# First weight pairs of an encoder layer: plain products per tile pair and row half in place of half-depth Strassen

## The chip, the cores and the metric

The kernel runs on one core of a Trainium2 chip. The core has a matrix engine (TensorE, in the profile PE, with PEld for its weight loads), three elementwise engines (VectorE or DVE, ScalarE or ACT, GpSimd or POOL), and SyncE (SP), which here issues nearly all DMA transfers. Each engine runs its own instructions strictly in the order in which the build laid them down and waits on semaphores for the others. Products accumulate in PSUM, which has eight banks of 128 x 512 f32; everything else lives in SBUF. The metric is the device time of one execution in microseconds.

## The reference

One encoder layer over 1024 rows of width 2048, f32. A conditioning vector c gives shift and scale (the modulation), x is normalised by row and modulated, and the result h is multiplied with two wide weight matrices, `w_in` (4608 columns) and `w_merge` (4096 columns). What follows (attention over a window, pooling, gates, the output product) is the same in both kernels.

```python
mod = jax.nn.silu(c) @ w_ada + b_ada
shift, scale, gate = jnp.split(mod, 3, axis=-1)
h = rmsnorm(x, pre_g) * (1.0 + scale[:, None]) + shift[:, None]
proj = h @ w_in
...
g = jax.nn.sigmoid(h @ w_merge + b_merge)
```

## The kernel before, in words

**Tiling.** h is held turned: tile k (of 16) holds 128 of the 2048 columns of h on the partitions, and row half s (0 or 1) holds 512 of the 1024 rows: `xT[k, s]`. Weights come as pairs of 128 columns ("a weight pair", 256 columns, `ORDER` lists 34 of them). The contraction over 2048 is done in two passes, first over tiles 0 to 7 (`PART[0]`, results go to `part_d` in DRAM), then over tiles 8 to 15. Within a pass, tiles 2j and 2j+1 form tile pair j, j = 0 to 3.

**One product is three.** f32 values are split in a rounded part hi and a rest lo (`split`, lines 94 to 99: ACT writes hi, DVE subtracts and writes lo), and a product is hi*hi + hi*lo + lo*hi: three TensorE instructions of 128 x 128 by 128 x 512.

**Strassen.** For a weight pair, the 2 x 2 blocks (two tile halves by two column halves of the weights; two tile halves by two row halves of h) are multiplied with seven products instead of eight (`strassen`, lines 210 to 296). Its moving operands are the seven names in `MOVING`: the blocks B11, B21, B22 of h and the sums T1 to T4. B12 only enters through sums. For all four j a weight pair takes 7 x 3 x 4 = 84 TensorE instructions.

**The ramp.** To begin before all of h is there, the first `RAMP` = 4 weight pairs are done in two halves: first over j = 0, 1 for four pairs (results to `ramp_d`), then over j = 2, 3 (`ramp_gen`, lines 531 to 534, and the loops at 577 and 585), where the first half's results are loaded as `parts` and added. From the fifth pair on (`pass1`, line 602) all four j are done in one go, interleaved with side work (further modulation on DVE, sums of `w_out`). 22 pairs stand in the first call of `pass1`, the rest in the second.

**What leads to h.** `fetch_rows_of_x(s)` loads 16 tiles of 128 rows x 512 columns for half s. `norm_rows(si)` squares and sums a row block's four tiles (two on ACT, two on DVE) and makes a diagonal matrix `turn` of 1/rms. `turn_rows(s)` multiplies x with it on TensorE, which turns and scales x in one step (128 x 128 products into banks named XT), and copies the banks to `xT`. The modulation for tile pair j is a product of silu(c) (`scz`) with a 2048 x 512 block of `w_ada`: 16 TensorE instructions, four of which can work side by side on 32-column groups of the array (`modulation`, lines 443 to 463; bank GEMV). Then ACT copies the bank (`acc`), four small products add the groups (`sum_columns`, bank PM), and DVE forms `modc`. `modulate` applies it to `xT`, and `fill(j)` makes the 14 operands of tile pair j out of it.

**Order.** `fetch_rows_of_x` for both halves, the first raw weights, then `w_ada` for j = 0, 1, 2 in their own slots of the pool `big` (`ada_slots`) and for j = 3 through the ring `xa` of five buffers (`ada_tile`, two 256 KB loads each). All are loads on SyncE's one queue, at most eight on their way at a time. `claim` writes one column of the operands' slots early on POOL, so that they are taken from the pool ahead of need. The products of the modulation for j = 2 and 3 run in steps of two tiles between the Strassen products, pinned in the order in which they are written (`keep_in_program_order`). PSUM banks go by tags: mm, sc, at with two banks each, z0 and z1 (`SEEDED`) with one.

Of the kernel before, what the change touches and what calls it, by code (L numbers as in the profile page):

```python
# [42 lines left out]
def encoder_layer(ctx: ExitStack, tc: tile.TileContext, x, c, table, w_ada, b_ada, pre_g,  # L43
# [80 lines left out]
    RAMP = 4  # L124
# [3 lines left out]
    ramp_d = [dram.tile([256, S], F32, name=f"ramp_d{i}") for i in range(RAMP)]  # L128
# [51 lines left out]
    def load_raws(w, n0, rows, js):  # L180

        raws = []
        nj = len(js)
        joint = wp.tile([P, 2, nj, 256], F32, tag="raw", name=uid("raw"), bufs=4) if nj < 4 else None
        for kh in range(2):
            r = joint[:, kh] if nj < 4 else wp.tile([P, nj, 256], F32, tag="raw", name=uid("raw"), bufs=4)
            load(r, rows(w, js, kh)[:, :, n0:n0 + 256])
            raws.append(r)
        return raws
# [20 lines left out]
    def strassen(w, n0, rows, js, op, ev, finish, part=None, raws=None, ahead=False):  # L210
# [56 lines left out]
        if ahead:  # L267
            wts = iter(list(wts))
            yield
# [75 lines left out]
    ev_ctx = ExitStack()  # L345
    ev = ev_ctx.enter_context(pool("ev1", 9, side="right"))
    early = ExitStack()
    ep = early.enter_context(pool("early", side="right"))
    rows = ev.tile([P, 512], F32, tag="ev", name="rows")[0:104, 0:P]
# [16 lines left out]
    xT = {}  # L366
    for s in range(2):
        for k in PART[0]:
            if k % 4 == 3:
                xT[k, s] = rp.tile([P, 512], F32, name=f"xT{k}_{s}")  # L370
            else:
                xT[k, s] = slot("xT", F32)
                nc.gpsimd.memset(xT[k, s][:, 0:1], 0.0)
    xts, turn = {}, {}
# [7 lines left out]
    def norm_rows(si):  # L382
        ssq = ep.tile([P, 8], F32, tag="ssq", name=f"ssq{si}", bufs=4)
        for q in range(4):
            xt = xts[si, q]
            if q < 2:
                junk = bank("sc", "junk")
                nc.scalar.activation(junk, xt, AF.Square, accum_out=ssq[:, q:q + 1])
            else:
                junk = bank("at", "junk")  # L390
                nc.vector.scalar_tensor_tensor(junk, xt, 1.0, xt, op0=ALU.mult, op1=ALU.mult,
                                               accum_out=ssq[:, q:q + 1])
# [3 lines left out]
        turn[si] = ep.tile([P, P], F32, tag="turn", name=f"turn{si}", bufs=8)  # L396
        nc.vector.tensor_scalar(turn[si], ident, rstd[:, si:si + 1], None, op0=ALU.mult)

    def turn_rows(s):

        for q in range(2):
            banks = [bank(t, "XT1") for t in ("mm", "mm", *SEEDED)]
            for m in range(4):
                for j in range(4):
                    nc.tensor.matmul(banks[j][:, m * P:(m + 1) * P], xts[4 * s + m, q][:, j * P:(j + 1) * P],
                                     turn[4 * s + m], start=True, stop=True)
            for j in range(4):
                if j % 2 == 0:
                    nc.vector.tensor_copy(xT[q * 4 + j, s], banks[j])
                else:  # L410
                    nc.scalar.activation(xT[q * 4 + j, s], banks[j], AF.Copy)
# [22 lines left out]
    def ada_slots(j):  # L434
        tiles = []
        for kc in range(KT):
            tiles.append(slot("ada", F32, (P, 4, P)))
            load(tiles[kc].rearrange("p (g h) n -> p g (h n)", g=2),
                 w_ada[kc * P:(kc + 1) * P, 0:2 * D].rearrange("p (g n) -> p g n", g=2)
                 [:, :, j * 256:(j + 1) * 256])  # L440
        return tiles

    def modulation(j, tile_of, pin=False):

        st_ = {}

        def step(q):
            if q == 0:
                st_["pv"] = bank("at", "GEMV")
            pv = st_["pv"]  # L450
            for kc in (2 * q, 2 * q + 1):
                g = kc % 4 * 32
                ins = nc.tensor.matmul(pv[g:g + 32, :], scz[:, kc, :], tile_of(kc), start=kc < 4,
                                       stop=kc >= 12, tile_position=(0, g))
                if pin:
                    tc.keep_in_program_order(ins)
            if q == 7:
                acc = xa2.tile([P, 4, P], F32, tag="acc", name=uid("acc"), bufs=2)
                tc.keep_in_program_order(
                    nc.scalar.activation(acc, pv.rearrange("p (g n) -> p g n", g=4), AF.Copy))  # L460
                mod_columns(j, sum_columns(acc))

        return [lambda q=q: step(q) for q in range(8)]
# [30 lines left out]
    def modulate(eng, t, k):  # L494
        j, kh = k // 2, k % 2
        if eng is nc.scalar:
            eng.activation(t, t, AF.Identity, scale=modc[:, 1, kh, j:j + 1], bias=modc[:, 0, kh, j:j + 1])
        else:
            eng.tensor_scalar(t, t, modc[:, 1, kh, j:j + 1], modc[:, 0, kh, j:j + 1],
# [7 lines left out]
    def claim(j):  # L507

        for name in MOVING:
# [875 lines left out]
```

## Time and profile before

| what | value |
|---|---|
| device time, three runs | 2154.8, 2163.8, 2165.83 us (median 2163.8) |
| span of the profiled execution, first to last instruction | 2152.0 us |
| TensorE busy | 2098.7 us, 98% |
| DVE, ACT busy | 1539.9 us, 1129.6 us |
| DMA moved | 466.11 MB, mean 217 GB/s |

The median of the runs is 11.8 us above the span of the profiled execution; the execution that was profiled lies within its span and what the runs add around it.

How to read the profile: a timeline row has start and duration in us, the engine, the line of the kernel, the instruction, what it writes <- what it reads, the shape and how many such instructions were merged (xN). In brackets stand the idle time before and what ended it. A row of a table by stretches gives, for each engine, busy us and in parentheses the number of instructions, then TensorE's granted clock (1.00 is full), the mean busy share of the DMA engines and what they moved. A matmul's own duration is longer than the distance to the next, because matmuls overlap; the distance between starts is what counts. f32 matmuls (turning x, modulation) show two records for each instruction, the products of split operands one.

### The profile page before, as it was taken

To read this page: it belongs to the slowest core of one execution; us is meant where nothing else is said; L and a number is where in the kernel's file an instruction comes from. 1 tells how busy PE (TensorE), PEld (TensorE's weight loads), DVE (VectorE), ACT (ScalarE), POOL (GpSimd) and SP (SyncE) were. 2 spreads that over 40 slices of the span, in tenths; PEclk is the share of its full clock that TensorE was granted. 3 is DMA by queue.
4 is the path that set the end of the run, shared out by engine and by line. 5 is a ranking of instruction groups with operands and counts; after the bars stand their busy time and mean duration, and the time that the engine had idled before them with its cause. 6 is when DMAs were issued, how large, how long until landed. Compare 5 with 4: busy or idle time off the path is not lost.

```text
span 2152.0 us, 28951 instructions
## 1 busy us (share of the span) xinstructions
PE 2098.7 (98%) x9567; PEld 1716.3 (80%) x9567; DVE 1539.9 (72%) x2754; ACT 1129.6 (52%) x2124; POOL 7.4 (0%) x66
## 2 busy tenths in 40 slices
PE   6999999999999999999999999999999999999998
PEld 4588888887878888888888887888788887878886
DVE  5786666776547676777776878566967877879666
ACT  5654444443474546767765443334645544757654
POOL 0000000000000000000000000000000000000000
PEclk9999999999999999999999999999999999999999
DMA  9986566898666355545445765755654655686996
GB/s 333 290 277 202 188 203 212 296 316 271 227 224 206 118 175 199 171 158 186 161 150 189 220 223 192 238 177 177 229 175 156 230 167 175 207 287 215 303 314 226
DMA packets 303255, 466.11 MB, mean 217 GB/s; under 512 B 23882, under 2 KB 144866, under 8 KB 303104
## 3 DMA queue, kind: packets, MB, share of 16 engines
q1 hardware_dynamic: 301648, 462.02, 65.3%
q0 software_dynamic: 1120, 2.19, 0.3%
q8 instruction: 75, 1.23, 0.2%
q14 instruction: 76, 0.62, 0.1%
q10 hardware_dynamic: 336, 0.06, 0.0%
HBM read 340.41 MB, written 125.85 MB: 217 GB/s over the span
## 4 chain that ended last, share of the span: by engine, by line
PE 84%; DMA 8%; DVE 4%; ACT 2%; issue 1%; SPq 1%; DVEq 0%; ACTq 0%
PE Z L235 28%; PE X L235 18%; PE V L235 18%; DMA raw<-in_w_merge_dram 3%; PE Z L1131 2%; PE Z L1132 2%; PE Z L1133 2%; PE V L1131 1%; PE V L1133 1%; PE V L1132 1%; PE X L1132 1%; PE X L1133 1%; PE X L1131 1%; DVE wlo L96 1%; DMA xt<-in_x_dram 1%
## 5 line engine op out<-in xcount | busy, mean ns | idle before, releaser
L95 ACT ACTIVATE whi<-raw 128x512 fp32r<-128x512 f32 (+1 forms) x528 | 320.2, 610 | 509.1 <-PE Z L235 265.3
L96 DVE TENSOR_TENSOR wlo<-raw,whi 128x512 fp32r<-128x512 f32 (+1 forms) x528 | 346.9, 662 | 191.4 <-PE Z L235 114.6
L96 DVE TENSOR_TENSOR wlo<-wr,whi 128x512 fp32r<-128x512 f32 x224 | 150.9, 689 | 62.5 <-ACT whi L95 57.7
L95 ACT ACTIVATE whi<-wr 128x512 fp32r<-128x512 f32 x224 | 138.1, 628 | 99.6 <-DVE wlo L96 35.3
L102 DVE TENSOR_TENSOR raw<-raw,raw 128x512 f32<-128x512 f32 x80 | 55.2, 690 | 95.1 <-DMA raw<-in_w_merge_dram 73.2
L235 PE MATMUL V<-T3h,whi 128*128 128x512 f32 x336 | 92.3, 393 | 6.2 <-DVE u L102 6.2
L1057 ACT ACTIVATE gt<-gt,cols 128x512 f32<-128x512 f32 x64 | 46.0, 723 | 99.0 <-DMA gt<-proj_d 74.1
L235 PE MATMUL X<-B11h,whi 128*128 128x512 f32 x336 | 92.5, 393 | 3.2 <-DVE part L102 1.9
L235 PE MATMUL Z<-B22h,whi 128*128 128x512 f32 x336 | 92.8, 395 | 0.9 <-ACT u L290 0.9
L235 PE MATMUL Z<-T1h,whi 128*128 128x512 f32 x336 | 91.8, 392 | 0.9 <-ACT T1h L95 0.9
L235 PE MATMUL V<-T4h,whi 128*128 128x512 f32 x336 | 92.2, 392 | 0.0
L235 PE MATMUL X<-B11l,whi 128*128 128x512 f32 x336 | 92.1, 393 | 0.2 <-DVE B11l L96 0.2
L235 PE MATMUL X<-B11h,wlo 128*128 128x512 f32 x336 | 91.5, 392 | 0.0
L235 PE MATMUL Z<-T2h,whi 128*128 128x512 f32 x336 | 91.3, 391 | 0.0
L235 PE MATMUL Z<-T1l,whi 128*128 128x512 f32 x336 | 91.0, 390 | 0.1
L235 PE MATMUL Z<-B22l,whi 128*128 128x512 f32 x336 | 90.9, 390 | 0.0
L235 PE MATMUL X<-B21h,whi 128*128 128x512 f32 x336 | 90.9, 390 | 0.0
L235 PE MATMUL V<-T3l,whi 128*128 128x512 f32 x336 | 90.9, 390 | 0.0
L235 PE MATMUL V<-T4l,whi 128*128 128x512 f32 x336 | 90.8, 390 | 0.0
L235 PE MATMUL V<-T4h,wlo 128*128 128x512 f32 x336 | 90.8, 389 | 0.0
L235 PE MATMUL Z<-T1h,wlo 128*128 128x512 f32 x336 | 90.7, 390 | 0.0
L235 PE MATMUL Z<-T2l,whi 128*128 128x512 f32 x336 | 90.7, 390 | 0.0
(306 smaller groups left out, 4849.9 us busy)
## 6 DMA issues: line engine op xcount, KB each, us to landing
part<-part_d SPq DMA_DIRECT2D x136, 256.0 KB, 4.9
ada<-in_w_ada_dram SPq DMA_DIRECT2D x128, 256.0 KB, 4.7
raw<-in_w_in_dram SPq DMA_DIRECT2D x64, 512.0 KB, 4.0
raw<-in_w_merge_dram SPq DMA_DIRECT2D x64, 512.0 KB, 5.7
wr<-ws_dS SPq DMA_DIRECT2D x64, 512.0 KB, 5.4
wr<-in_w_out_dram SPq DMA_DIRECT2D x48, 512.0 KB, 5.2
proj_d<-part SPq DMA_DIRECT2D x68, 256.0 KB, 2.2
sw<-in_w_out_dram SPq DMA_DIRECT2D x64, 256.0 KB, 5.4
```

The costliest lines, as they stand in the source:

```text
L95: ins = (nc.scalar.activation(hi, src, AF.Copy), nc.vector.tensor_tensor(lo, src, f32(hi), ALU.subtract))
L96: nc.vector.tensor_tensor(lo, src, f32(hi), ALU.subtract))
L102: return (eng or nc.vector).tensor_tensor(o, a, b, ALU.add)
L235: nc.tensor.matmul(ps, w_[:, i], op[mov][j][m_], start=fresh and i == 0 and n == 0, stop=i == nj - 1 and n == 2, skip_group_check=True)
L1057: nc.scalar.activation(gt, gt, AF.Sigmoid, bias=cols[:, col:col + 1])
L1131: nc.tensor.matmul(pb, hi, w[0], start=first, stop=False, skip_group_check=True)
L1132: nc.tensor.matmul(pb, lo, w[0], start=False, stop=False, skip_group_check=True)
L1133: nc.tensor.matmul(pb, hi, w[1], start=False, stop=last, skip_group_check=True)
```

## The change

Two weight pairs instead of four form the ramp, and they are done with plain products, eight blocks instead of seven, as soon as one tile pair j of one row half s is there. Four accumulations take the place of the halves: U0 (pair 0, s = 0) in the banks z0, z1, U1 (pair 0, s = 1) in mm, U2 (pair 1, s = 1) in sc, each over j = 0 to 3; U3 (pair 1, s = 0) is done for j = 0 at once and put by in `ramp_d`, and for j = 1 to 3 at the end, with the stored part added. Each takes 2 x 3 x 2 = 12 instructions for each j.

```diff
-    RAMP = 4
+    RAMP = 2
...
+    def plain(i, j, s, banks, first, last):
+
+        hi, lo = plain_w[i, j]
+        mov = (op["B11"][j], op["B21"][j]) if s == 0 else (b12s[j], op["B22"][j])
+        for nt in range(2):
+            for n, (w_, m_) in enumerate(((hi, 0), (hi, 1), (lo, 0))):
+                for kh in range(2):
+                    nc.tensor.matmul(banks[nt], w_[:, kh, nt * P:(nt + 1) * P], mov[kh][m_],
+                                     start=first and n + kh == 0, stop=last and n == 2 and kh == 1,
+                                     skip_group_check=True)
```

`fill` is cut in two: `put_blocks(j, s)` modulates and splits the plain blocks of a row half, `put_sums(j)` makes the sums T1 to T4 later, one j behind. B12 is split too (pool `ramp`, two buffers). The modulation takes four tiles a step and fetches all of its tiles through the ring `xa`; `ada_slots`, `claim`, `ramp_gen`, the OPEN products and the `ahead` argument of `strassen` go. The products of the modulation are pinned for every j.

```diff
-            for kc in (2 * q, 2 * q + 1):
+            for kc in range(4 * n, 4 * n + 4):
                 g = kc % 4 * 32
...
-        return [lambda q=q: step(q) for q in range(8)]
+        return fetch, [lambda n=n: step(n) for n in range(4)]
```

`norm_rows` squares two tiles on DVE into a scratch tile and two on ACT in place, where before ACT took the first two and DVE the last two, into PSUM. `turn_rows(s, ks, tags)` turns chosen tiles into chosen banks; tiles 0 and 1 are modulated while they are copied out of the bank. The order of the start:

```diff
+    mods = [modulation(j) for j in range(4)]
     fetch_rows_of_x(0)
+    for q in range(8):
+        mods[0][0](q)
+    fetch_raws([0])
+    for si in range(4):
+        norm_rows(si)
+    turn_rows(0, (2, 3, 4, 5), ("sc", "sc", *SEEDED))
+    turn_rows(0, (6, 7), ("sc", "sc"))
+    for step in mods[0][1]:
+        step()
+    turn_rows(0, (0, 1), ("mm", "mm"))
     fetch_rows_of_x(1)
+    fetch_raws([1])
+    put_blocks(0, 0)
...
+    plain(0, 0, 0, u0, True, False)
...
+    plain(1, 0, 0, u3, True, True)
...
+    for si in range(4, 8):
+        norm_rows(si)
+    for q in range(8):
+        mods[1][0](q)
...
+    plain(1, 0, 1, u2, True, False)
...
+    plain(0, 0, 1, u1, True, False)
+    for step in mods[1][1]:
         step()
+    units = ((0, 0, u0), (0, 1, u1), (1, 1, u2))
+    for j in range(1, 4):
+        if j < 3:
+            for q in range(8):
+                mods[j + 1][0](q)
+        for s in range(2):
+            put_blocks(j, s)
+        for i in range(RAMP):
+            put_plain(i, j)
+        put_sums(j - 1)
+        side = deque(mods[j + 1][1] if j < 3 else ())
+        for n, (i, s, banks) in enumerate(units):
+            plain(i, j, s, banks, False, j == 3)
+            for _ in range(1 + n // 2):
+                if side:
+                    side.popleft()()
```

The build may move instructions of an engine past each other where nothing is pinned. As built, on TensorE the modulation product for j = 1 stands behind U1's products for j = 0, and each later modulation's small PM products stand directly ahead of the next j's plain products. On SyncE the loads of the ring's first five tiles for j = 1 stand ahead of and behind the second half of x, and the sixth to eighth behind the first raw weights of the third pair. `pass1` now begins with the third pair (`i = RAMP`); everything behind it is unchanged.

238 lines of the change are left out of this document (110 added, 128 removed).

## The prediction

> **What bounds the kernel now.** I read the page's totals first, then the busy time in stretches of 20 us over the start, then TensorE's timeline there, and last who TensorE waited for after the start. First the totals, and TensorE's busy tenths in 40 slices of the span.
>
> ```profile
> span 2152.0 us, 28951 instructions
> PE 2098.7 (98%) x9567; PEld 1716.3 (80%) x9567; DVE 1539.9 (72%) x2754; ACT 1129.6 (52%) x2124; POOL 7.4 (0%) x66
> PE   6999999999999999999999999999999999999998
> ```
>
> TensorE is busy for 2098.7 of 2152.0 us, and nine tenths or more in all slices but the first and the last: what shortens or delays TensorE's queue moves the end. The stretches of the start (us, then busy us and instructions of each engine, granted clock, share of DMA):
>
> ```profile
> core 0: us, PE busy (x) PEld busy (x) DVE busy (x) ACT busy (x) POOL busy (x), PEclk, DMA share, GB/s
> 0.00:20.00 20.00, 3.87 (x17) 3.65 (x18) 8.71 (x33) 11.50 (x29) 1.10 (x18) 1.00 0.85 289
> 20.00:40.00 20.00, 17.64 (x116) 14.03 (x116) 13.63 (x41) 9.50 (x27) 1.35 (x14) 0.91 1.08 366
> 40.00:60.00 20.00, 18.72 (x96) 6.21 (x95) 11.25 (x22) 9.14 (x16) 1.49 (x14) 1.00 1.10 349
> 60.00:80.00 20.00, 19.32 (x81) 9.09 (x82) 15.19 (x33) 13.00 (x25) 0.00 (x0) 1.00 1.05 337
> 80.00:100.00 20.00, 20.00 (x86) 11.93 (x85) 14.59 (x31) 12.84 (x27) 0.00 (x0) 1.00 0.71 223
> 100.00:120.00 20.00, 20.00 (x90) 16.55 (x89) 16.85 (x37) 15.18 (x33) 0.00 (x0) 1.00 0.94 302
> ```
>
> The DMA share is full until 80 us, while TensorE turns x and takes modulation products; the weight products only come into their stride later. From 100 us TensorE has no gap. What it waits for behind the start, in total, times and longest:
>
> ```profile
> PE V L235 <- DVE u L102: 6.2, 3, 3.3
> PE X L1132 <- DVE ml L96: 3.9, 1, 3.9
> PE b L745 <- ACT xt L739: 3.5, 2, 2.0
> ```
>
> These are some 14 scattered us in a later part whose instructions the change leaves in their order; only the place of two weight pairs shifts (ORDER stays, the first pass starts at pair 2 instead of pair 4). So the question is at what time TensorE, having done the same work, enters the gapless part. TensorE's timeline where the ramp ends (start, duration, operation, count):
>
> ```profile
> 152.15 1.07 PE L235 MATMUL X<-B11h,whi 128*128 128x512 f32 x4
> ...
> 153.06 0.67 PE L235 MATMUL Z<-B22h,whi 128*128 128x512 f32 x2
> ...
> 154.49 1.09 PE L235 MATMUL X<-B11l,whi 128*128 128x512 f32 x4
> ...
> 156.32 1.07 PE L235 MATMUL V<-T3h,whi 128*128 128x512 f32 x4
> ...
> 159.04 1.07 PE L235 MATMUL Z<-T2h,whi 128*128 128x512 f32 x4
> ```
>
> Twelve products (T3, three rows of four, 156.32 to 159.04) take 2.72 us: 0.2267 us each. At 152.15 the first four products of the first full pair slip in (0.91), then the ramp's last B22 products run to 154.49; the ramp's end, with those four taken off, is 153.6. Before has by then done four pairs, after will have done two. Two whole pairs are 2 x 84 x 0.2267 = 38.1 us. **The break-even is therefore a ramp that ends at 115.5 us.** Each us later is a us on the end.
>
> **The change on TensorE, in work.** For two pairs 2 x 96 = 192 plain products stand where Strassen needed 2 x 84 = 168: 24 x 0.2267 = 5.4 us more; the two OPEN products go (0.5 less). The 64 products that turn x stay. The modulation products stay 64, but in steps of four tiles:
>
> ```profile
> 36.81 3.84 PE L405 MATMUL XT<-turn,xt 128*128 128x128 f32 x32
> 40.58 3.62 PE L453 MATMUL GEMV<-ada,scz 128*32 128x512 f32 x26
> 44.89 1.05 PE L424 MATMUL PM<-ones,acc 128*128 128x1 f32 x8 [0.69 <-ACT acc L460]
> ...
> 65.41 1.07 PE L453 MATMUL GEMV<-ada,scz 128*32 128x512 f32 x8
> 67.53 1.05 PE L453 MATMUL GEMV<-ada,scz 128*32 128x512 f32 x4
> ```
>
> Eight records (four tiles) last from 65.41 to 66.41, and four records (two tiles) from 67.53 to 68.52: the same 0.99 us. A modulation in four steps costs 4.0 us of TensorE instead of 8 x 0.99 = 7.9. Between 60 and 94 us that saves about 6 us. By work alone (+5.4, -0.5, -6) the change is even. It is decided by waits.
>
> **The change as a chain of waits.** The new instruction order is fixed by the build, so I walk it with the durations of before. These are the rows:
>
> ```profile
> 1.23 22.42 SPq L380 DMA_DIRECT2D xt<-in_x_dram  x32
> 24.68 35.79 SPq L438 DMA_DIRECT2D ada<-in_w_ada_dram  x47
> 18.94 0.73 DVE L391 SCALAR_TENSOR_TENSOR junk<-xt 128x512 f32<-128x512 f32 x1
> ...
> 20.55 0.29 DVE L397 TENSOR_SCALAR turn<-ident,rstd 128x128 f32<-128x128 f32 x1
> 15.78 0.58 ACT L388 ACTIVATE junk<-xt 128x512 f32<-128x512 f32 x1
> 22.17 1.08 ACT L411 ACTIVATE xT<-XT 128x512 f32<-128x512 f32 x2 [1.24 <-PE XT L405]
> 44.24 0.60 ACT L460 ACTIVATE acc<-GEMV 128x512 f32<-128x512 f32 x1 [2.85 <-PE GEMV L453]
> 45.98 0.17 DVE L428 TENSOR_TENSOR modc<-PM,cols 128x4 f32<-128x4 f32 x1 [4.67 <-PE PM L424]
> 46.37 1.52 ACT L497 ACTIVATE xT<-xT,modc 128x512 f32<-128x512 f32 x2 [1.54 <-DVE modc L431]
> 47.80 0.62 ACT L95 ACTIVATE B11h<-xT 128x512 fp32r<-128x512 f32 x1
> DMA to landing us min/median/max: 2.9/5.9/6.3
> ```
>
> SyncE's loads: 32 row tiles of x in 22.42 us, 0.70 each; 47 modulation loads in 35.79, 0.76 each, the queue full both times. The last tile of x's first half is squared at 18.94; I take 18.5 as landed, and 20.6 for its turn matrix.
>
> (1) Behind those tiles stand nine loads of w_ada (25.3), the raw weights of tile pairs 0 and 1 and three of four of the rest (1.8 MB, seven loads' worth: 30.7), and w_ada's last six for j=0, whose buffers are free by then: 35.2. GEMV ends 35.5. From a GEMV's end to modulation before took 44.20 to 46.37, 2.2 us (ACT acc, PM, modc): 37.7.
>
> (2) Four loads more, then the second half of x: from 38.3 a tile each 0.70, the twelfth at 46.7, the last at 49.5. On ACT the six squares of that half stand ahead of the split B11h, so it ends at 46.7 + 0.6 + 0.6 = 47.9, although its input was modulated at 38.5; DVE's B21l, behind the thirteenth tile's square, at 49.8. U0 and the first U3, 24 products, run to 54.6.
>
> (3) Then turning and plain products alternate on the two mm banks: 32 turning products at 3.84/16 = 0.24 (7.7) and 24 products of U2 and U1 (5.4) make 67.7. Each batch waits for its banks to be copied out; none before, so bounded: 0 if all hidden, 5 if four batches wait two 0.6 us copies each. I take 1.2, since other products lie between: 68.9.
>
> (4) Here is the costly step. The ring xa has five double tiles, a modulation eight. Tile 6 of j=1 may load only when the GEMV has read tile 1, and this GEMV stands behind U1 in TensorE's order. SyncE issues it at 69.2, and behind it on that queue wait all later w_ada. Landing takes 2.9 us at the least and 5.9 in the full queue; DMA is idle by then, so 3.0, and five more at 0.76: 76.0. GEMV ends at 76.3. If the queue were full, 3 us more.
>
> (5) Now three rounds in which nothing covers the chain from GEMV to split: 2.2 to modulation, 2.05 from there to B11h (46.37 to 47.80 + 0.62). So 4.25, three times, TensorE waiting. Each of the first two rounds has 36 products (8.2) and four GEMV steps (4.0), 12.2; their last three tiles are fetched after step one, early enough. 80.6, 92.8, 97.0, 109.2, 113.5; the last 36 products with 0.2 of gating end at 121.9, the 36 of U3 at **130.0**.
>
> (6) The clock. Before shows it at half once near the start (0.50 in one stretch of 2 us, 0.82 to 0.83 in its neighbours: some 3.4 us in all), not at all around a gap of 3.3 us after 500 us, and for about twice as long around a gap of 3.9 us after 1820 us:
>
> ```profile
> 30.00:32.00 2.00, 1.45 (x10) 1.26 (x9) 1.59 (x6) 0.91 (x3) 0.30 (x3) 0.83 1.10 350
> 32.00:34.00 2.00, 2.00 (x7) 0.85 (x6) 1.58 (x8) 0.82 (x3) 0.19 (x2) 0.50 1.10 347
> 34.00:36.00 2.00, 2.00 (x11) 1.11 (x12) 1.42 (x4) 0.65 (x2) 0.10 (x1) 0.82 1.12 352
> 500.00:510.00 10.00, 6.70 (x30) 5.21 (x29) 8.65 (x12) 3.19 (x6) 0.00 (x0) 1.00 0.82 277
> 1820.00:1830.00 10.00, 5.85 (x21) 4.12 (x21) 9.79 (x17) 2.73 (x6) 0.00 (x0) 0.84 0.63 196
> 1830.00:1840.00 10.00, 10.00 (x38) 8.12 (x37) 8.86 (x16) 6.67 (x13) 0.00 (x0) 0.82 0.42 141
> ```
>
> After idles for 10 us ahead of U0, then 4 to 5 us four times. A window of 3.4 us at half speed costs 1.7 us of products. Bounds: none, 0; five gaps with a window each, 8.5, or with two each, 17. I take one window, since the products behind most gaps wait for their splits anyway: 131.7.
>
> The Trainium skill (TensorE: Matmul & The Clock Gate, "HAM oscillation — how this bites in real kernels") says that a TensorE gap beyond about 3.4 us drops it to half rate. Taken at its word for all five gaps the ramp would end at 138.5, not 131.7; the trace agrees at 500 and at 1820 us, but behind the idle first stretch (3.87 us busy of 20) the low clock came only at 30 us.
>
> **The other edits.** The squares of x change engines (ACT 0.58, DVE 0.73 each, eight and eight as before, no bank needed); the first two tiles of x are modulated while they are copied out, one pass of 0.5 to 0.8 us less ahead of (2), where ACT is held by the squares anyway; the 40 memsets of claim go from POOL, on which nothing waits. Costed at nothing too: 14 of 16 parts loaded from ramp_d, 14 of 16 stores, 40 ACT and 74 DVE instructions fewer (they lie under TensorE: DVE 16.85 of 20 us from 100 to 120, TensorE 20.00); the sums T1 to T4, one round late (without U3's 8.2 us over the last, up to 8 us). U3's evacuation waits for parts of ramp_d, queued on SyncE behind the stores of U0 to U2, which have only two buffers: two landings in turn at 2.9 from the end of U2's products on, 121.9, are over before U3 ends; at 5.9 each the next pair's Z bank would come 4 us late.
>
> **Sum.** 131.7 - 115.5 = +16.2: a span of 2168.2. The runs' median lies 11.8 above the profiled span; so **2180**, 0.75% slower.
>
> **Rivals.** *The waits are hidden, no loss.* If tile 6 were fetched under U0 and the three chains were covered, TensorE alone would bound from 47.9 on: 192 products 43.5, 32 turning 7.7, twelve steps 11.9, three PM 3.0: 114.0, that is -1.5, 2162. For it: idle DMA from 57 us on. Against: the order on TensorE, in which GEMV j=1 comes after U1 and U j after PM j. It decides by the gaps: none of 4 us between U0 and U3. It is also the floor of the ramp: a gain over 0.5% (10.8 us, about what a measurement here can tell) needs 104.7, out of its reach. Chance 0.06.
>
> *The late fetch is partly hidden:* TensorE gets through the alternation without copies waiting and the tail's loads land under the turning: ramp 124, or the two pairs that move into the second pass cover most of the 9.7 us that TensorE waits later behind u (6.2) and xt (3.5). +8, 2172. For: those waits are for DVE and ACT, which have fewer instructions. Against: the side steps keep their places in the pairs. Chance 0.22.
>
> *The clock falls at each gap,* 138.5, with two windows each 147: +23 to +31, 2187 to 2195. For: the gap after 1820 us, no longer than these. Against: the one after 500 us, and splits that bound the products behind a gap. It decides by the granted clock between 47 and 130 us. Chance 0.17.
>
> **How the numbers follow.** Forecast 0.55, 2176 to 2187: the alternation takes 1.2 off or adds 3.8, the full queue adds 3, the clock takes 1.7 off, and loads of w_ada at x's 0.70 take 1.6 off (26 loads in (1) and (2)). All but the first two rivals are slower than 0.5%: 0.55 and 0.17, with a little of the second: 0.74. Same 0.23, faster 0.03 (noise on the first). The range reaches into both neighbours: 2166 to 2192.
>
> **What would show it.** Right: B11h's first split near 48 us behind squares of x; on SyncE a w_ada load that waits for a GEMV near 69, and a DMA trough ahead of it; gaps of about 4 us before U0 in rounds two and three; the first full pair's X near 130. Wrong: that X before 120, U products through 70 to 80, or the difference lying behind 150 us.

## The result, and the profile after

| | device time (median, range) | ratio to before, 95% interval |
|---|---|---|
| before, 6 runs | 2161.0 us (2154.8 to 2166.2) | |
| after, 6 runs | 2181.7 us (2180.5 to 2184.1) | 1.0101 (1.0087 to 1.0115) |

The change makes the kernel 1% slower. The forecast was 2180. Read by its steps the forecast is less good than its total, so the profile after is read along them. The profiled execution of after took 2182.96 us with a span of 2181.2; before's span was 2152.0, so the two profiles differ by 29.2 us. First the stretches of 20 us behind 40 us (the same view as before's first table in the prediction: TensorE's busy time, then the other engines, granted clock, DMA share, GB/s):

```profile
40.00:60.00 20.00, 10.90 (x44) 8.59 (x45) 10.45 (x35) 10.78 (x29) 0.00 (x0) 0.66 0.85 309
60.00:80.00 20.00, 17.19 (x98) 10.71 (x97) 8.56 (x15) 3.90 (x8) 0.00 (x0) 1.00 0.38 111
80.00:100.00 20.00, 16.79 (x69) 10.19 (x72) 9.41 (x18) 7.00 (x13) 0.00 (x0) 0.83 0.60 201
100.00:120.00 20.00, 16.79 (x75) 10.07 (x68) 8.64 (x16) 6.27 (x11) 0.10 (x1) 0.83 0.77 251
120.00:140.00 20.00, 16.79 (x70) 11.37 (x69) 12.37 (x22) 11.01 (x20) 0.00 (x0) 0.83 0.71 229
140.00:160.00 20.00, 20.00 (x90) 16.57 (x89) 11.89 (x19) 7.56 (x13) 0.00 (x0) 1.00 0.71 220
```

Where before had TensorE busy for 18.7 to 20.0 of each 20 us from 40 us on, after has 10.9 to 17.2 until 140. Idle time is one part of the loss. The other is in the clock column: 0.66 and three times 0.83. DMA falls to 0.38 from 60 to 80. TensorE's timeline shows the place of each gap (start, duration, operation, count; in brackets the idle time ahead and what ended it):

```profile
38.08 1.05 PE L411 MATMUL PM<-ones,acc 128*128 128x1 f32 x8 [0.69 <-ACT acc L439]
48.45 0.80 PE L542 MATMUL U<-B11h,cwh 128*128 128x512 f32 x1 [9.32 <-ACT B11h L95]
...
56.92 1.95 PE L388 MATMUL XT<-turn,xt 128*128 128x128 f32 x16
...
71.48 2.77 PE L435 MATMUL GEMV<-ada,scz 128*32 128x512 f32 x20
75.27 1.91 PE L435 MATMUL GEMV<-ada,scz 128*32 128x512 f32 x4 [1.02 <-DMA ada<-in_w_ada_dram]
78.51 3.36 PE L435 MATMUL GEMV<-ada,scz 128*32 128x512 f32 x8 [1.33 <-DMA ada<-in_w_ada_dram]
82.56 1.05 PE L411 MATMUL PM<-ones,acc 128*128 128x1 f32 x8 [0.69 <-ACT acc L439]
...
86.14 1.22 PE L542 MATMUL U<-B11h,cwh 128*128 128x512 f32 x2 [2.52 <-ACT B11h L95]
...
99.66 3.12 PE L435 MATMUL GEMV<-ada,scz 128*32 128x512 f32 x16
...
107.04 1.22 PE L542 MATMUL U<-B11h,cwh 128*128 128x512 f32 x2 [2.52 <-ACT B11h L95]
...
128.00 1.22 PE L542 MATMUL U<-B11h,cwh 128*128 128x512 f32 x2 [2.53 <-ACT B11h L95]
...
146.75 1.07 PE L232 MATMUL X<-B11h,whi 128*128 128x512 f32 x4
```

The first full pair's X comes at 146.75: that is after's ramp end, against the break-even of 115.5 and a forecast of 131.7. All four gaps ahead of a first U product end with ACT's split B11h. From the end of j=1's GEMV (78.51 + 3.36 = 81.87) to 86.14 it is 4.27 us. SyncE's queue (start, duration of the issues, count) has the late fetch:

```profile
58.84 0.38 SPq L185 DMA_DIRECT2D raw<-in_w_in_dram  x1
72.58 6.96 SPq L404 DMA_DIRECT2D ada<-in_w_ada_dram  x12
```

After the load at 58.84 nothing is issued until 72.58, when the GEMV behind U1 has read its first tile. From then on the transfers are many, so the 0.38 of the 20 us stretch is a mean of an idle and a full part (the same view, 4 us):

```profile
76.00:80.00 4.00, 2.67 (x7) 0.41 (x6) 0.00 (x0) 0.00 (x0) 0.00 (x0) 1.00 0.94 256
```

And the clock, in steps of 2 us around the gap at 84 us:

```profile
84.00:86.00 2.00, 0.00 (x0) 0.00 (x0) 1.02 (x3) 1.95 (x4) 0.00 (x0) 0.77 1.09 383
86.00:88.00 2.00, 1.86 (x4) 1.50 (x5) 1.88 (x4) 2.00 (x5) 0.00 (x0) 0.50 0.40 138
88.00:90.00 2.00, 2.00 (x6) 1.60 (x5) 2.00 (x5) 1.73 (x4) 0.00 (x0) 0.50 0.00 0
90.00:92.00 2.00, 2.00 (x6) 1.52 (x6) 2.00 (x4) 0.00 (x0) 0.00 (x0) 0.52 0.00 0
92.00:94.00 2.00, 2.00 (x13) 0.72 (x12) 1.43 (x3) 0.00 (x0) 0.00 (x0) 1.00 0.00 0
```

The clock drops some 1.1 us ahead of the first product and stays at half, worked out from the column, for 0.9 + 2 + 2 + 1.9 = 6.8 us; 5.8 of them fall on products, 13 of the 15 that follow. Read in steps of 1 us, it falls at 85.1, 105.6 and 126.0 us, each time for 6.8 us. The falls are 20.5 us apart, the rounds 20.9: a fall does not come at a fixed distance from its gap, but 1.1, 1.5 and 2.0 us ahead of the first product. Ahead of U0 it falls at 40.7 and comes back at 54.4, 5.9 us into the products.

### The profile page after: what moved, and what is told of

It reads as the page before. It is cut to its first block, busy times and chain, and to the rows that moved or that the text cites. A ratio compares the mean times of both kernels' runs of the same rounds, so it can differ in the third digit from the quotient of the medians.

```text
span 2181.2 us, 28637 instructions
## 1 busy us (share of the span) xinstructions
PE 2110.4 (97%) x9589; PEld 1730.7 (79%) x9589; DVE 1513.9 (69%) x2680; ACT 1117.9 (51%) x2084; POOL 4.2 (0%) x26
## 4 chain that ended last, share of the span: by engine, by line
PE 85%; DMA 7%; DVE 4%; ACT 2%; issue 1%; SPq 0%; DVEq 0%; ACTq 0%; POOL 0%; POOLq 0%
PE Z L232 27%; PE V L232 18%; PE X L232 18%; PE U L542 3%; PE Z L1164 2%; PE Z L1165 2%; PE Z L1166 2%; PE X L1165 1%; PE X L1166 1%; PE X L1164 1%; DMA xt<-in_x_dram 1%; PE V L1165 1%; PE V L1164 1%; PE V L1166 1%; DVE wlo L96 1%
## 5 line engine op out<-in xcount | busy, mean ns | idle before, releaser
L95 ACT ACTIVATE whi<-raw 128x512 fp32r<-128x512 f32 (+1 forms) x500 | 311.1, 625 | 511.6 <-PE Z L232 255.0
L96 DVE TENSOR_TENSOR wlo<-raw,whi 128x512 fp32r<-128x512 f32 (+1 forms) x500 | 338.4, 682 | 205.1 <-PE Z L232 132.4
L232 PE MATMUL Z<-T2h,wlo 128*128 128x512 f32 x328 | 87.9, 390 | 0.0
L232 PE MATMUL X<-B21l,whi 128*128 128x512 f32 x328 | 87.9, 390 | 0.0
L232 PE MATMUL V<-T3h,wlo 128*128 128x512 f32 x328 | 87.8, 390 | 0.0
```

The costliest lines, as they stand in the source:

```text
L95: ins = (nc.scalar.activation(hi, src, AF.Copy), nc.vector.tensor_tensor(lo, src, f32(hi), ALU.subtract))
L96: nc.vector.tensor_tensor(lo, src, f32(hi), ALU.subtract))
L232: nc.tensor.matmul(ps, w_[:, i], op[mov][j][m_], start=fresh and i == 0 and n == 0, stop=i == nj - 1 and n == 2, skip_group_check=True)
```

## The experiments

The theory after this reading: the loss lies in the ramp alone, in (a) the late fetch for j=1, (b) the three uncovered chains, (c) the half clock behind each gap, and (d) the late U0. The rivals: the steps of four tiles or the 24 extra products, a clock that falls for other reasons, or loads that bound the ramp in any order. The ramp end below is the start of the first X behind U3; the kernels with two pairs in the ramp compare directly. Times are medians; the last column is the ratio to before with its 95% interval, each to runs of before taken beside it (medians 2159.8 to 2161.8 us).

| kernel | ramp end, us | time, us | ratio to before |
|---|---|---|---|
| after | 146.75 | 2181.7 | 1.0101 (1.0087 to 1.0115) |
| early steps | 138.40 | 2175.8 | 1.0072 (1.0049 to 1.0096) |
| fillers | 139.27 | 2172.1 | 1.0052 (1.0031 to 1.0073) |
| two-tile steps | 145.87 | 2182.6 | 1.0112 (1.0086 to 1.0138) |
| pinned splits | 153.21 | 2189.2 | 1.0124 (1.0109 to 1.0140) |
| splits first | 144.94 | 2184.4 | 1.0127 (1.0102 to 1.0152) |
| covered chains | 128.11 | 2163.2 | 1.0010 (1.0001 to 1.0019) |
| pinned and covered | 136.61 | 2174.6 | 1.0049 (1.0033 to 1.0066) |
| splits first, covered | 127.95 | 2165.0 | 1.0026 (1.0013 to 1.0040) |
| the same, loads held | 123.63 | 2159.6 | 1.0001 (0.9984 to 1.0019) |
| the same, fillers at U0 | 123.10 | 2162.2 | 1.0013 (0.9997 to 1.0029) |

### Four-tile steps alone, on the kernel before

```diff
-            for kc in (2 * q, 2 * q + 1):
+            for kc in range(4 * q, 4 * q + 4):
...
-            if q == 7:
+            if q == 3:
...
-    for _ in range(3):
+    for _ in range(2):
         side.popleft()()
...
-        run(ramp_gen(0, i, None) if i else gen, side, range(7),
+        run(ramp_gen(0, i, None) if i else gen, side, (0, 2, 4, 6),
```

> The kernel before, with its four Strassen pairs in the ramp, and only the modulation steps of j=2 and j=3 in fours (8 steps among the products where 16 stood). Theory (the loss of the change sits in the waits of the new ramp, and the four-tile steps by themselves are a gain): ramp end about 6 us earlier than before's 153.6, 147 to 149, time 4 to 7 us below before. Rival A (the steps of before hid behind the full DMA queue, so that fewer of them gain nothing): ramp end 152 to 154.5, time the same within 2 us. Rival B (back-to-back groups of four tiles cost as much as two single steps, and bunch the loads): ramp end later than 155.

Measured: 2158.1 us, ratio 0.9997 (0.9980 to 1.0013). TensorE's timeline of this kernel:

```profile
63.08 1.67 PE L453 MATMUL GEMV<-ada,scz 128*32 128x512 f32 x8
...
72.08 3.21 PE L453 MATMUL GEMV<-ada,scz 128*32 128x512 f32 x8 [0.43 <-DMA ada<-in_w_ada_dram]
...
83.81 1.05 PE L453 MATMUL GEMV<-ada,scz 128*32 128x512 f32 x2
...
156.41 1.09 PE L235 MATMUL X<-B11l,whi 128*128 128x512 f32 x4
```

The second rows of X at 156.41, less the four early X products (0.91), give a ramp end of 155.5, 1.9 us later than before's 153.6 by the same count. The gain of 6 us falls. Ahead of 76 us groups of eight records take 1.67 and 3.21 us in place of 1.07, the second with a wait for its tiles in brackets, and behind it the build breaks some steps into pieces of one tile (x2), each of which takes 1.05 us like a whole step. By its ramp end this is the last rival, by its time no change.

### Two of j=1's steps early

```diff
-    for ks in ((2, 3), (4, 5), (6, 7)):
+    for n, ks in enumerate(((2, 3), (4, 5), (6, 7))):
         turn_rows(1, ks, ("mm", "mm"))
+        if n < 2:
+            mods[1][1][n]()
...
-    for step in mods[1][1]:
+    for step in mods[1][1][2:]:
         step()
```

> The changed kernel, with the first two of j=1's four modulation steps taken between the batches that turn x instead of behind U1. Theory (the tiles 6 to 8 of j=1 are fetched late because the ring is freed behind U1): SyncE's wait until 72.6 goes, j=1's GEMV ends at 75.5 to 77 instead of 81.9, everything behind it moves with it: ramp end 140.5 to 142.5 instead of 146.75, time 4 to 6 us below the changed kernel. Rival (DMA is the bound there and the tiles land no earlier, or the steps hold up the turning): GEMV end 80 or later, ramp end 145 to 148.

Measured: 2175.8 us, 5.9 below after; ramp end 138.40. SyncE's queue and TensorE's timeline:

```profile
64.34 13.40 SPq L404 DMA_DIRECT2D ada<-in_w_ada_dram  x16
```

```profile
63.22 1.07 PE L435 MATMUL GEMV<-ada,scz 128*32 128x512 f32 x8
66.20 1.06 PE L435 MATMUL GEMV<-ada,scz 128*32 128x512 f32 x8
72.66 1.92 PE L435 MATMUL GEMV<-ada,scz 128*32 128x512 f32 x16
```

The loads go out at 64.34 in place of 72.58, and the last two steps find their tiles: 1.92 us for 16 records, no wait, GEMV end 74.6 in place of 81.9. The late fetch is shown, and it was a matter of where the GEMV stood in TensorE's order. Of the 8.4 us at the ramp end, 1.1 are there already when the turning of x's second half begins (55.87 for 56.92), so some 7.3 are the edit's. The same two steps took 3.12 us at 99.66 in after; their own wait for tiles is the likely reason, but no run isolates it.

### Fillers in the gaps of the rounds

```diff
+    def fill_clock(n):
+        fb = bank("at", "FILL")
+        hi = op["B11"][0][0]
+        for _ in range(n):
+            keep(nc.tensor.matmul(fb, hi[:, 0:P], hi, start=True, stop=True))
...
-                mod_columns(j, sum_columns(acc))
+                if j:
+                    fill_clock(3)
+                pm = sum_columns(acc)
+                if j:
+                    fill_clock(11)
+                mod_columns(j, pm)
```

> The changed kernel, with 3 products of 128x512 that nothing reads put on TensorE between each GEMV's end and PM, and 11 between PM and the next round's first product, for j = 1 to 3 (42 products, 9.5 us of work laid into the gaps). Theory (the granted clock falls to half because TensorE idles some 4 us at each round, and this costs 2.2 to 2.9 us a round): granted clock 1.00 from 84 to 146 us, first products of each round at 0.227 instead of 0.427 us, the gap itself unchanged in length, ramp end 138 to 140 instead of 146.75, time 6 to 9 us below the changed kernel. Rival A (the clock falls for another reason, as the time since the last fall): clock 0.83 in these stretches as before, ramp end 146 to 149. Rival B (the fillers run past the splits and push the products back): ramp end 148 or later at a full clock.

Measured: 2172.1 us, 9.6 below after, with 42 products more; ramp end 139.27. Timeline, then a 20 us stretch:

```profile
81.42 0.96 PE L418 MATMUL FILL<-B11h 128*128 128x512 f32 x3
82.22 1.01 PE L411 MATMUL PM<-ones,acc 128*128 128x1 f32 x8
83.09 2.77 PE L418 MATMUL FILL<-B11h 128*128 128x512 f32 x11
85.77 0.73 PE L553 MATMUL U<-B11h,cwh 128*128 128x512 f32 x2
```

```profile
80.00:100.00 20.00, 20.00 (x97) 11.26 (x95) 9.42 (x18) 7.27 (x14) 0.00 (x0) 1.00 0.73 236
```

The gap is as long as it was (81.49 to 85.77, 4.28 us), but the clock stays at 1.00 and the 15 products behind it take 3.7 us in place of 6.3. So it is the gap, and not the time since the last fall or the products behind it, that takes the clock down. It costs 2.6 us in this round. From the first U product of round one to the ramp end it is 53.5 us (85.77 to 139.27) in place of 60.6 (86.14 to 146.75): 7.1 us in the three.

### Two-tile steps again

```diff
-            for kc in range(4 * n, 4 * n + 4):
+            for kc in (2 * n, 2 * n + 1):
...
-            plain(i, j, s, banks, False, j == 3)
-            for _ in range(1 + n // 2):
-                if side:
-                    side.popleft()()
+            plain(i, j, s, banks, False, j == 3, side, (1 + n // 2,) * 2)
```

`plain` takes that many steps behind each of its two half units.

> The changed kernel with modulation in steps of two tiles again, spread over the half units of rounds one and two (1, 1, 1, 1, 2, 2 instead of four tiles each behind the units 1, 1, 2). Theory (a two-tile step costs as much as a four-tile one): each of these two rounds has 2 steps more of about 1 us, so 2 to 3 us a round, ramp end 150 to 153, time 3 to 6 us above the changed kernel. Rival (two steps back to back cost 3.1 us, so steps of two that stand alone cost no more than half of it): ramp end 145 to 148, time the same within 2 us.

Measured: 2182.6 us, ramp end 145.87, both within 1 us of after, as the rival has it. The rounds say otherwise. They take 21.2 and 22.4 us (84.24, 105.42, 127.80) in place of 20.9 and 21.0, and the clock was not the same in both kernels. The stretches of this one:

```profile
80.00:100.00 20.00, 16.82 (x70) 8.97 (x70) 9.41 (x18) 7.00 (x13) 0.00 (x0) 0.91 0.62 208
100.00:120.00 20.00, 16.68 (x67) 8.74 (x70) 8.64 (x16) 6.27 (x11) 0.10 (x1) 0.83 0.74 237
120.00:140.00 20.00, 16.68 (x77) 12.02 (x70) 12.55 (x22) 11.62 (x21) 0.00 (x0) 0.91 0.63 212
```

In rounds one and three the clock was at half for some 3.4 us (0.91) where after has 6.8 (0.83). In round two it was at half for 6.8 us in both kernels, and there the steps of two tiles make the round 1.4 us longer: six groups of 1.05 to 1.08 us (6.35) stand in place of 1.06, 1.07 and 3.31 (5.44). By these two profiles the grouping is therefore worth something, less than the 2 to 3 us a round of the theory; the equal time came from a clock that was at half for less long, and from turning that began 1.2 us earlier (55.76 for 56.92).

### Splits of j=0 held ahead of x's squares, two forms

First form: the splits B11 and B21 of j=0 are pinned, and so is each square of x's second half. Second form (splits first): also `norm_rows(4..7)` is written directly behind `put_blocks(0, 0)`, since a pinned instruction goes behind the one written before it on its engine.

```diff
-            put(op, "B11", j, t1)
-            put(op, "B21", j, t2)
+            put(op, "B11", j, t1, j == 0)
+            put(op, "B21", j, t2, j == 0)
...
+            if si >= 4:
+                keep(ins)
```

The second form adds:

```diff
     put_blocks(0, 0)
+    for si in range(4, 8):
+        norm_rows(si)
...
-    for si in range(4, 8):
-        norm_rows(si)
     for q in range(8):
         mods[1][0](q)
```

> The changed kernel, with the splits B11 and B21 of j=0 held ahead of the squares of x's second half on ACT and DVE (order only). Theory (U0 starts at 48 only because ACT has squares that wait for x's loads ahead of the split, and its first products run at half clock because TensorE idled 9.3 us): first U product at 40.5 to 42.5 instead of 48.45 with a gap of about 2.5 us, first U products at 0.227 us, x's second half turned from 50 to 52 on instead of 56.9, ramp end 140.5 to 143, time 4 to 6 us below the changed kernel. Rival (loads behind x set the pace, so what is won ahead of U0 is waited for at j=1's modulation): GEMV of j=1 still ends near 81.9 and the time is the same within 1.5 us.

> The changed kernel with the splits B11 and B21 of j=0 ahead of the squares of x's second half on ACT and DVE, as in the run with pinned splits, but with the squares directly behind the splits and ahead of the evacuation of U3 (in the earlier run they fell behind that evacuation and behind a split that waited for a raw weight, which cost 17 us at the turning of x). Theory (the order on ACT alone keeps U0 until 48): U0 at 40.5, x's second half turned from 51 to 53 instead of 56.9, ramp end 141 to 144, time 3 to 6 us below the changed kernel. Rival (the late tiles of w_ada stand behind U3's stores and raw weights on SyncE, and what is won ahead of U0 is lost there): GEMV j=1 ends at 80 or later, time the same within 1.5 us.

Measured: the first form 2189.2 us, ramp end 153.21, the second 2184.4 us, 144.94. U0 came at 40.6 and 40.2 as wanted, and nothing was won. The second form's timelines on TensorE and on DVE:

```profile
40.21 0.80 PE L544 MATMUL U<-B11h,cwh 128*128 128x512 f32 x1 [1.93 <-ACT B11h L95]
...
57.37 1.22 PE L390 MATMUL XT<-turn,xt 128*128 128x128 f32 x4 [7.38 <-DVE turn L383]
```

```profile
55.49 0.69 DVE L105 TENSOR_TENSOR ws<-raw 128x512 f32<-128x512 f32 x1 [5.32 <-DMA raw<-in_w_in_dram]
56.10 0.15 DVE L378 TENSOR_REDUCE ssq<-ssq 128x1 f32<-128x4 f32 x1
```

A sum for the first full pair's weights stands on DVE ahead of the last row block's reduction and waits 5.32 us for its load, so the last row block of tiles 0 and 1 is turned at 57.37, as late as in after. Neither theory nor rival had this: not SyncE's queue but an in-order DVE took the gain. The ramp end 1.8 us below after's is no gain of the order either: j=1's GEMV ends 1.0 us later (82.89 for 81.87), and behind it the granted clock is 0.91 in each of the stretches from 80 to 140 us where after has 0.83. In the first form the squares fell behind U3's evacuation on ACT, and x was turned some 8 us later still (last row block at 65.66).

### Covered chains

The early steps, and each last pair of steps moved ahead of a unit of 12 products:

```diff
         turn_rows(1, ks, ("mm", "mm"))
+        if n < 2:
+            mods[1][1][n]()
+    for step in mods[1][1][2:]:
+        step()
     u1 = [bank("mm", "U1") for _ in range(2)]
     plain(0, 0, 1, u1, True, False)
-    for step in mods[1][1]:
-        step()
...
         for n, (i, s, banks) in enumerate(units):
-            plain(i, j, s, banks, False, j == 3)
             for _ in range(1 + n // 2):
                 if side:
                     side.popleft()()
+            plain(i, j, s, banks, False, j == 3)
```

> The changed kernel with j=1's first two modulation steps between the turning batches (as in the run that took them early), and each j's last two steps ahead of a unit of 12 products instead of behind it, so that this unit lies over the chain from the GEMV's end to the split. Theory (the three chains of 4.3 us and the half clock behind them are what the changed kernel loses in the rounds): each gap ahead of a round's first product falls from 2.5 us (4.3 with ACT's 0.7 and PM) to under 1 us, the granted clock stays at 1.00 behind 60 us, a round takes 14 to 16 us instead of 20.9, ramp end 120 to 125, time 18 to 24 us below the changed kernel, that is 2158 to 2164, level with before. Rival A (the loads of w_ada bound the rounds: 4.2 MB each at 340 to 350 GB/s are 12.4 us, and the ring frees late): GEMV waits for DMA in each round, rounds of 17 us or more, ramp end 129 or later. Rival B (the last unit delays PM and modulation): gaps of over 1.5 us stay.

Measured: 2163.2 us, 18.5 below after, ratio to before 1.0010. Stretches and two rows of the timeline:

```profile
80.00:100.00 20.00, 19.50 (x103) 11.00 (x99) 13.89 (x27) 11.83 (x24) 0.00 (x0) 1.00 0.84 268
100.00:120.00 20.00, 18.50 (x90) 11.98 (x83) 13.91 (x25) 9.52 (x18) 0.10 (x1) 1.00 0.75 249
```

```profile
96.12 0.73 PE L542 MATMUL U<-B11h,cwh 128*128 128x512 f32 x2 [0.50 <-ACT B11h L95]
...
111.57 0.73 PE L542 MATMUL U<-B11h,cwh 128*128 128x512 f32 x2 [1.50 <-ACT B11h L95]
```

A round takes 15.4 us (80.74, 96.12, 111.57), the gaps fall to 0.5 and 1.5 us, the clock stays full, and the loads keep up. Against the early steps alone, which this kernel contains, the covering is worth 10.3 us of ramp and 12.7 us of time. The ramp end, 128.1, is 3 us later than expected, of which 1.1 is there at 49.58 already, where this execution's U0 starts (48.45 in after).

### Both together, and the loads held back

> Both edits in one: the splits of j=0 ahead of the squares, and the covered chains. Theory: the two gains add, ramp end 115 to 120, time 2152 to 2160, level with before or up to 0.3% below. Rival (the pinned splits win nothing since j=1's loads come no earlier): as the covered kernel alone, within 1.5 us.

> The same splits-first order together with the covered chains. Theory: both gains add, ramp end 121 to 125 instead of 128.1 with covered chains alone, time 2157 to 2161, level with before. Rival (with the chains covered the loads set the pace): TensorE waits for w_ada in j=1's GEMV and the ramp end stays at 127 to 129, time as with covered chains alone, 2163.

Measured: the first form of the splits with covered chains 2174.6 us, ramp end 136.61; the second form 2165.0 us, 127.95. The kernels combine the edits shown. The second form is the rival's case by its time, though not by a wait for w_ada: the last row block of tiles 0 and 1 is turned at 57.34. Against the covered chains alone (128.11) the first form loses 8.5 us of ramp (6.5 without them), the second gains nothing. So the DVE wait was removed: the first full pair's raw weights are loaded in round j=3, and the weight splits of j=1 to 3 follow the split B22 of j=0.

```diff
+        if j == 3:
+            first = []
+            w, n0 = weight_of(ORDER[RAMP])
+            for kh in range(2):
+                first.append(wp.tile([P, 4, 256], F32, tag="raw", name=uid("raw"), bufs=4))
+                keep(load(first[kh], rows_in_turn(0)(w, range(4), kh)[:, :, n0:n0 + 256]))
...
-        for i in range(RAMP):
-            put_plain(i, j)
+        with tc.issue_after(b22[0].ins), tc.issue_after(b22[1].ins):
+            for i in range(RAMP):
+                put_plain(i, j)
```

The last kernel adds fillers around PM of j=0 (`fill_clock` here with products of 128x256 on j=0's weights, which are split ahead of it):

```diff
-                mod_columns(j, sum_columns(acc))
+                if j == 0:
+                    fill_clock(6)
+                pm = sum_columns(acc)
+                if j == 0:
+                    fill_clock(16)
+                mod_columns(j, pm)
```

> The covered chains with the splits of j=0 first, and two things moved that held up x's turning in the run before: the raw weights of the first full pair are loaded in round j=3 (so its sums do not stand on DVE, waiting 5.3 us for that load, ahead of the last row block's turn matrix), and the weight splits of j=1 to 3 follow the split B22 of j=0. Theory (what was won ahead of U0 was lost to DVE and ACT instructions that wait for loads in front of the last turn matrix): the last batch of the first two tiles of x is turned at 50 to 52.5 instead of 57.3, ramp end 121 to 124.5 instead of 128.0, time 4 to 6 us below the kernel with splits first and covered chains, 2157 to 2160, level with before. Rival (the w_ada loads of j=1 set the pace there, so TensorE only waits later): GEMV of j=1 waits for DMA over 2 us, ramp end 126 or later, time the same within 2 us.

> As the run above, with 6 products of 128x256 that nothing reads between j=0's GEMV and PM and 16 between PM and U0. Theory (U0 and U3 run at half clock until 44.5 because TensorE idles around PM ahead of them): granted clock 1.00 from 38 to 48, 24 products in 5.5 us instead of 8.1, and since x's turning waits for x's loads anyway the ramp end moves by 0 to 1 us only. Rival (the clock falls there because of the thin modulation steps from 31 to 36 already): clock still about 0.5 from 38 to 44.

Measured: loads held 2159.6 us, ratio 1.0001 (0.9984 to 1.0019), ramp end 123.63. The last row block of x is turned at

```profile
52.35 0.71 PE L392 MATMUL XT<-turn,xt 128*128 128x128 f32 x4 [1.54 <-DVE turn L385]
```

5 us earlier than with splits first and covered chains, and 4.3 of them arrive at the ramp end; which of the two moves did it was not tried apart. With the fillers at U0 as well the clock stays full there, as the theory has it. Stretches without fillers (loads held) and with them:

```profile
42.00:44.00 2.00, 2.00 (x6) 1.44 (x6) 1.85 (x6) 0.91 (x4) 0.00 (x0) 0.50 1.04 393
...
50.00:60.00 10.00, 7.81 (x44) 6.70 (x46) 6.79 (x18) 6.13 (x17) 0.00 (x0) 0.83 0.50 179
```

```profile
42.00:44.00 2.00, 1.92 (x9) 1.54 (x9) 1.60 (x6) 0.78 (x4) 0.00 (x0) 1.00 1.05 403
...
50.00:60.00 10.00, 7.77 (x31) 6.45 (x30) 6.38 (x17) 5.86 (x17) 0.00 (x0) 0.66 0.54 193
```

The 24 products take 6.2 us (40.85 to 47.05) in place of 8.1 (41.22 to 49.31), x's turning waits for x anyway, and the ramp ends 0.5 us earlier. The clock falls later instead, while x is turned: 0.66 from 50 to 60 us is 6.8 us at half, 0.83 without the fillers 3.4. The time, 2162.2, is not distinguishable from the run without (the intervals overlap). No version is shown to be faster than the kernel before.

### The kernel before once more

> The kernel before, unchanged, for a second profile of it. Its runs spread over 2150 to 2170 us, and its first profiled execution was among the shorter ones (span 2152.0), so the ramp of the change costs 29 to 31 us by the two profiles and only 21 by the medians. Theory (the spread comes from gaps behind 440 us, each of which the clock punishes in some executions and not in others): ramp end 153.0 to 154.5 again, and whatever the span is above 2152 lies behind 440 us, in stretches with a granted clock of 0.90 to 0.98 and in gaps of some us. Rival (the start itself varies): the ramp end moves by as much as the span does.

Measured: 2161.9 us in its one execution, span 2160.1, ramp end 153.7. Of the 8.1 us by which this span exceeds the first profile's, only 0.1 lies in the ramp. Both profiles, first the earlier one, then this one, behind 440 us:

```profile
440.00:760.00 320.00, 311.66 (x1414) 255.72 (x1413) 206.62 (x316) 160.83 (x316) 2.28 (x3) 1.00 0.68 225
...
1840.00:2140.00 300.00, 293.97 (x1288) 240.82 (x1287) 227.44 (x367) 191.75 (x363) 0.00 (x0) 1.00 0.80 265
```

```profile
440.00:760.00 320.00, 311.34 (x1399) 255.22 (x1398) 203.33 (x310) 158.57 (x312) 2.27 (x3) 0.99 0.68 223
...
1840.00:2140.00 300.00, 292.64 (x1269) 240.07 (x1268) 225.59 (x362) 191.65 (x359) 0.00 (x0) 0.99 0.82 265
```

Fewer instructions are done in these stretches, at 0.99 in place of 1.00; in the two between them, the second profile does 8 fewer and 12 more. Read in fine steps, the clock of the second is at half six times for 3.4 us between 440 and 2150 us, that of the first once for 3.4 and once for 6.8: 20.5 us in place of 10.2. Over the whole span (totals on the page) TensorE is busy for 2103.8 in place of 2098.7 us with the same 9567 instructions, and idle for 56.3 in place of 53.3: 5.1 us more of products and 3.0 of waits. The theory holds: the start is the same, and the spread lies behind it. At 31 us the first profile has 3.4 us of half clock that the second does not have, and the ramp ends at the same time, so there it cost nothing.

## Why the prediction was right, and where it was not

The time (2181.7 for 2180) and the direction were right, the places of the waits were right, and the total came out because two mis-sized terms nearly cancel, which is luck.

- **Break-even 115.5.** Right as an account of the profile. After's ramp ends 31.2 us above it, its span is 29.2 us longer.
- **(1), (2): U0 near 48 behind the squares.** B11h was done at 48.4 for 47.9. The products of U0 and U3 ended at 56.9 for 54.6, the first 5.9 us of them at half clock.
- **(3): the alternation, 14.3 us.** Measured 14.6 (56.92 to 71.48).
- **(4): the late fetch.** Shown by the early steps. Its size was the term with an open bound: 7.4 us forecast if the DMA queue is idle, 3 more if full; measured 10.4 (71.48 to 81.87). The queue was idle up to the issue, but the twelve loads that then went out one behind the other filled it (0.94 from 76 to 80 us), so the upper bound was the right one.
- **(5): the chains, 4.25 us each.** Measured 4.27, shown by the covered chains. The body of a round was forecast at 12.2 us and took 16.6: 2.6 of the difference is the clock (fillers), 1.1 the last two steps (3.12 for 1.98); 0.7 is not assigned.
- **(6): the clock. This term failed.** One window of 3.4 us was charged for all gaps, 1.7 us. In after each of the three gaps in the rounds brought 6.8 us at half, 4.9 to 5.8 of them on products; together they cost 7.1 us (fillers). U0's cost about 1.9, if the 24 products of the kernel with fillers at U0 stand for it (8.1 us in place of 6.2). That is the third rival's mechanism. That the ramp end, 146.75, meets its upper value of 147 is luck: its clock term is 17 us, and some 9 were paid; the late fetch (3.0) and the longer bodies of the rounds made up most of the rest. The reason given for not taking it, that products behind a gap wait for their splits anyway, was wrong: behind the gap they ran back to back at 0.427 us in place of 0.227.

  How long the half clock lasts behind such a gap is not fixed. The five kernels without covered chains or fillers have three gaps of 4.3 to 4.4 us each. In after and with early steps all three brought 6.8 us; with two-tile steps the second did and the other two brought 3.4; with pinned splits and splits first all six brought 3.4. Read in steps of 1 us, the seven falls that brought 6.8 us came 1.1 to 2.3 us ahead of the first product, the eight that brought 3.4 came 0.6 us ahead or later. So one window at a gap, as charged, does occur, but at every gap, and after had two each time.

  The Trainium skill (TensorE: Matmul & The Clock Gate, "HAM oscillation — how this bites in real kernels") has a gap beyond about 3.4 us drop the rate to half. These gaps, of 0.69 and 2.52 us with only PM's eight 128x1 records between, agree with it; the trace adds, as I read it, that such thin work does not count as busy.
- **The work: four-tile steps save 6 us.** Wrong: nothing on the kernel before, and on after 1.4 us in the one round in which the clocks can be compared. On the kernel before, groups took longer than the 1.07 us of a whole step or were broken up; that ready loads would have brought the 6 us is not shown.
- **The sum: 11.8 us around the span. This term failed too.** It came from setting before's profiled span against the median of other executions. In all six runs of after, time and span differ by 1.7 to 1.8 us; before's profiled execution must have taken some 2154 and was one of its shorter ones. So a span 13.0 us too short and a supplement 10.0 us too long gave 2180: that the total is so close is luck.

The range held. What remains open: by the ramp ends after loses 31 us to before, by the medians 21, and the kernel with held loads is level in time with its ramp 8 us behind the break-even. Before's second profile has 8 us more behind the ramp than its first, so its typical execution is likely slower there than the one that the break-even was taken from. Why the versions with two pairs in the ramp show this less was not tried.

## What to carry to other kernels

Count the gaps that a change opens on TensorE, and price each with half speed for 3.4 or 6.8 us from about its end on (both occurred here), besides its own length; 12 products laid over the chain were worth far more than the instructions that the change saved. When an instruction is moved forward in time, look at every in-order engine on its path for one that waits for a load in front of the next link. When two kernels with such gaps are compared, compare the granted clock of their stretches too: two-tile steps looked free because the clock was at half for less long. And set a predicted span against the profiled execution's own time, and take the spread of the runs as a range of its own.

## What the runs showed of the hardware

- At a gap of 4.3 us (0.69 and 2.52 us idle, eight 128x1 records between) the clock went to half in all 15 such gaps of five kernels, for 3.4 or for 6.8 us; 6.8 came when the fall was 1.1 us or more ahead of the first product behind the gap, 3.4 when it was 0.6 us ahead or later.
- 14 products that nobody reads, laid into the gap, kept the clock at 1.00: 7.1 us at the ramp end and 9.6 us of device time in three rounds.
- A group of modulation products on 32-column parts takes 1.05 to 1.08 us alone, be it two, four or eight records; sixteen back to back take 1.92 when their tiles are there.
